# A list scheduler and GpSimd substitution in the first phase of a hybrid decoder layer

## The chip, the core and the metric

The program runs on one core of a Trainium2 chip. A core has TensorE (matrix products and transposes, results in PSUM), VectorE, ScalarE, GpSimd and SyncE, which here only issues DMA. Each engine works its own queue in program order; semaphores tie the queues together. The metric is the device time of one launch in microseconds.

## The reference, cut

One decoder layer over 2048 tokens of width 1024. Its input projection has 26 tiles of 128 columns, for two groups of heads: eight RWKV-7 heads of 64 and four gated-linear-attention (GLA) heads. A SwiGLU feed-forward of width 2816 follows.

```python
def reference(x, rms1_g, w_in, ..., final_g):
    h = x
    for l in range(DEPTH):                      # DEPTH = 1
        n = rms_norm(h, rms1_g[l])
        z = n @ w_in[l]
        y_rwkv = rwkv7_mixer(z[..., :D_RWKV_IN], ...)
        y_gla = gla_mixer(z[..., D_RWKV_IN:], gk_up[l], gk_bias[l], gla_norm_g[l])
        mix = jnp.concatenate([y_rwkv, y_gla], axis=-1).astype(h.dtype)
        h = h + mix @ w_out[l]
        n = rms_norm(h, rms2_g[l])
        h = h + (jax.nn.silu(n @ ffn_gate[l]) * (n @ ffn_up[l])) @ ffn_down[l]
    return rms_norm(h, final_g)

# rwkv7_mixer, per token and head: the state S is 64 x 64
    sa = jnp.einsum('bhvk,bhk->bhv', S, a_t)
    S = (S * w_t[:, :, None, :] + sa[..., None] * b_t[:, :, None, :]
         + v_t[..., None] * k_t[:, :, None, :])
    y = jnp.einsum('bhvk,bhk->bhv', S, r_t)
```

Both kernels take the recurrence in chunks of 64 tokens: inside a chunk a triangular system (I - E) X = R is solved, and the state goes from chunk to chunk.

## The kernel before

Phase A works on four blocks of 512 tokens. In a block the rows are normed and transposed (`nprep`), split into a high and a low part, and multiplied with 26 tiles of the input projection (`zmm`, three matmuls for each of eight slices of the channels, L381 to L383; result `zd`). The weights of a tile come by DMA and are split by ScalarE (`w_hi`, L371) and GpSimd (`w_lo`, L372), twice 512 columns each.

Two heads lie on the 128 partitions together, so a block has four head pairs, sixteen in all. Each goes through three streams:

- `stage_a`: decay, keys, scores. Its masked scores are `e` (L539) and `ra` (L541).
- `stage_a2`: solves the triangular systems. Four 32-partition transposes (L597) spread the diagonal 32 x 32 blocks of `e` into `ln`; 31 steps of a multiply and an add (L606, L608) on VectorE invert them into `lm`, the sizes from 31 columns over 76 down to 8; a transpose makes `ui` (L626). Six groups of small matmuls and the moves of their results follow (`xu` L640, `xy` L648, `xl` L657, two of each); VectorE adds `xy` to `R` (L653), ScalarE copies the others (L644, L661). At the end `ar` is written (L667).
- `stage_b`: the chain over eight chunks. For each: matmul `yp` (L693), VectorE `uv` (L695), matmul `ch` (L700), VectorE `S` (L703, two halves), and so on to the next chunk. Then group norm and gate.

The GLA group has `glaz` and `gmix`. Five Python generators are merged by `run` (a heap ordered by time estimates that the generators give as they yield), and the scheduler of the framework then orders the instructions of each engine by its own estimates; once built, the order is fixed. PSUM has the tags `zd`, `ma` and `mb` with two banks each and `yp` and `ch` with one.

Phase B is the output projection with residual (L964 to L966) and the feed-forward (`up`, `down`), in three matmuls for each product, too. In its first part it uses what phase A leaves free.

## Time and profile before

| | us |
|---|---|
| median of 3 runs | 3006.15 |
| lowest, highest | 3003.69, 3013.07 |
| span of the profiled execution, first to last instruction | 3011.3 |
| last matmul of the input projection starts | 1282.4 |
| last state step of `stage_b` (L703) starts | 1361.0 |

The profiled execution has no other time than its span; the span is within the range of the three runs and 5 us above their median. In the rows below, busy time is the time in which an engine shows at least one instruction; for TensorE the ends of matmuls are modelled, so starts are safer than ends. PEld is TensorE's weight load. The granted clock is given as a share of full speed: TensorE has two levels, 1.2 and 2.4 GHz, so a number between 0.5 and 1.0 is a mixture of both over the stretch.

### The profile page before, as it was taken

How to read it: one execution, taken by the hardware profiler on the slowest of the kernel's cores; microseconds unless marked ns; L12 is line 12 of the kernel's file. 1: busy time of each engine (PE TensorE's matmuls, PEld its weight loads, DVE VectorE, ACT ScalarE, POOL GpSimd, SP SyncE). 2: the span in 40 equal slices, each digit the busy share in tenths (PEclk: the TensorE clock that was granted, in tenths of full speed). 3: DMA queues.
4: the chain of work that ended last, by engine and by line, in shares of the span. 5: the costliest groups of instructions: out<-in, count | busy, mean ns of one | idle time of the engine just before them, and what ended most of it. 6: DMA issues, size and time to landing. Idle time of an engine off the chain costs nothing.

```text
span 3011.3 us, 38996 instructions
## 1 busy us (share of the span) xinstructions
PE 2871.0 (95%) x15112; PEld 2247.0 (75%) x15112; DVE 1732.7 (58%) x3990; ACT 953.1 (32%) x1718; POOL 344.2 (11%) x451
## 2 busy tenths in 40 slices
PE   7898999899898989899999999999999999999998
PEld 5676677666666767668878888888888888888886
DVE  6868797888888897874433333333355333333334
ACT  5444445444445445332321111111132111111112
POOL 4222232213322222200000000000000000000000
PEclk9999989989999999989999999999999999999999
DMA  3122111221122111135531111111134111111111
GB/s 108 48 71 78 50 53 47 78 67 56 53 67 81 53 53 50 57 114 175 180 119 45 54 42 42 50 55 50 42 126 138 52 42 42 51 54 50 42 42 57
DMA packets 99033, 206.08 MB, mean 68 GB/s; under 512 B 8608, under 2 KB 41600, under 8 KB 98848
## 3 DMA queue, kind: packets, MB, share of 16 engines
q1 hardware_dynamic: 98848, 203.59, 21.7%
q8 instruction: 119, 1.95, 0.3%
q14 instruction: 66, 0.54, 0.1%
HBM read 178.39 MB, written 25.17 MB: 68 GB/s over the span
## 4 chain that ended last, share of the span: by engine, by line
PE 76%; DVE 20%; issue 2%; ACT 1%; DMA 1%; POOL 0%; SPq 0%; DVEq 0%; ACTq 0%; POOLq 0%
PE ups L995 5%; PE ups L996 5%; PE gps L996 5%; PE gps L997 5%; PE gps L995 5%; PE ups L997 5%; PE dn L1018 5%; PE dn L1019 5%; PE dn L1017 5%; DVE ln L597 3%; PE zd L383 3%; DVE lm L608 3%; PE zd L381 3%; PE zd L382 3%; DVE lt L606 3%
## 5 line engine op out<-in xcount | busy, mean ns | idle before, releaser
L381 PE MATMUL zd<-nh,w_hi 128*128 128x512 f32 x832 | 353.9, 426 | 0.8 <-DVE gkk L777 0.6
L383 PE MATMUL zd<-nh,w_lo 128*128 128x512 f32 x832 | 349.2, 420 | 0.0
L1020 DVE TENSOR_TENSOR h<-dn,h 128x512 f32<-128x512 f32 x352 | 242.7, 690 | 180.6 <-PE dn L1019 180.5
L382 PE MATMUL zd<-nl,w_hi 128*128 128x512 f32 x832 | 345.6, 415 | 0.0
L372 POOL TENSOR_TENSOR w_lo<-w_raw,w_hi 128x512 fp32r<-128x512 f32 x208 | 273.8, 1322 | 614.5 <-ACT w_hi L371 571.8
L1000 DVE TENSOR_TENSOR sgu<-sgu,ups 128x512 f32<-128x512 f32 x88 | 60.2, 684 | 392.6 <-PE ups L997 390.4
L1018 PE MATMUL dn<-wdl,hh 128*128 128x512 f32 x704 | 278.4, 395 | 0.0
L996 PE MATMUL gps<-n2l,wgh 128*128 128x512 f32 x704 | 278.2, 395 | 0.0
L995 PE MATMUL gps<-n2h,wgh 128*128 128x512 f32 x704 | 277.6, 394 | 0.4 <-ACT wgh L901 0.4
L996 PE MATMUL ups<-n2l,wuh 128*128 128x512 f32 x704 | 278.0, 395 | 0.0
L995 PE MATMUL ups<-n2h,wuh 128*128 128x512 f32 x704 | 277.7, 394 | 0.2 <-ACT wuh L901 0.2
L1019 PE MATMUL dn<-wdh,hl 128*128 128x512 f32 x704 | 277.7, 395 | 0.0
L997 PE MATMUL gps<-n2h,wgl 128*128 128x512 f32 x704 | 277.4, 394 | 0.0
L997 PE MATMUL ups<-n2h,wul 128*128 128x512 f32 x704 | 277.4, 394 | 0.0
L1017 PE MATMUL dn<-wdh,hh 128*128 128x512 f32 x704 | 277.4, 394 | 0.0
L901 ACT CAST wdh<-raw 128x1024 fp32r<-128x1024 f32 x44 | 46.4, 1053 | 462.5 <-PE dn L1019 250.5
L383 PEld LDWEIGHTS zd<-nh,w_lo 128*128 128x128 f32 x832 | 161.6, 194 | 35.7 <-issue 7.5
L381 PEld LDWEIGHTS zd<-nh,w_hi 128*128 128x128 f32 x832 | 162.5, 195 | 33.2 <-issue 5.2
L382 PEld LDWEIGHTS zd<-nl,w_hi 128*128 128x128 f32 x832 | 161.9, 195 | 33.3 <-issue 7.9
L371 ACT CAST w_hi<-w_raw 128x512 fp32r<-128x512 f32 x208 | 126.3, 614 | 130.9 <-PE zd L382 83.7
L999 ACT ACTIVATE sgu<-gps 128x512 f32<-128x512 f32 x88 | 52.7, 599 | 339.4 <-PE gps L997 339.4
L995 PEld LDWEIGHTS gps<-n2h,wgh 128*128 128x128 f32 x704 | 132.1, 188 | 33.0 <-ACT wgh L901 0.9
(244 smaller groups left out, 5111.9 us busy)
## 6 DMA issues: line engine op xcount, KB each, us to landing
w_raw<-in_win SPq DMA_DIRECT2D x208, 256.0 KB, 2.7
raw<-in_wg SPq DMA_DIRECT2D x44, 512.0 KB, 4.2
raw<-in_wu SPq DMA_DIRECT2D x44, 512.0 KB, 3.6
raw<-in_wd SPq DMA_DIRECT2D x44, 512.0 KB, 3.6
xk<-in_x SPq DMA_DIRECT2D x16, 512.0 KB, 4.6
raw<-mix SPq DMA_DIRECT2D x16, 512.0 KB, 3.6
hx<-in_x SPq DMA_DIRECT2D x16, 512.0 KB, 3.6
hs<-hx SPq DMA_DIRECT2D x16, 512.0 KB, 2.9
```

The source lines that it names most:

```text
L371: nc.scalar.copy(out=whi[:, ks, :], in_=raw)
L372: nc.gpsimd.tensor_tensor(out=wlo[:, ks, :], in0=raw, in1=whi[:, ks, :].bitcast(F32), op=ALU.subtract)
L381: nc.tensor.matmul(out=ps, lhsT=whi[:, k, :], rhs=self.nh[k], start=(k == 0), stop=False)
L382: nc.tensor.matmul(out=ps, lhsT=whi[:, k, :], rhs=self.nl[k], start=False, stop=False)
L383: nc.tensor.matmul(out=ps, lhsT=wlo[:, k, :], rhs=self.nh[k], start=False, stop=(k == KT - 1))
L995: nc.tensor.matmul(out=ps, lhsT=w[0][:, ks], rhs=h, start=(k == 0), stop=False)
L996: nc.tensor.matmul(out=ps, lhsT=w[0][:, ks], rhs=l, start=False, stop=False)
L997: nc.tensor.matmul(out=ps, lhsT=w[1][:, ks], rhs=h, start=False, stop=(k == KT - 1))
L1017: nc.tensor.matmul(out=ps, lhsT=hh[:, ts], rhs=wd[f][0][:, ds], start=(f == 0), stop=False)
L1018: nc.tensor.matmul(out=ps, lhsT=hh[:, ts], rhs=wd[f][1][:, ds], start=False, stop=False)
L1019: nc.tensor.matmul(out=ps, lhsT=hl[:, ts], rhs=wd[f][0][:, ds], start=False, stop=(f == 1))
L1020: nc.vector.tensor_tensor(out=H[t][:, ds], in0=ps, in1=H[t][:, ds], op=ALU.add)
```

## The change

Three things are done together, all in phase A.

**The order.** `Order` replaces `run` and the framework's scheduler for this phase (`tc.manual_schedule()`). It emits nine streams: `b`, `a2`, `e` (results of the projection out of PSUM), `w` (weights), `x` and `p` (rows, normed and transposed), `a`, `g`, and `z` (projection matmuls) as the filler. After each emitted piece it reads the new instructions, gives each a duration by a formula for engine, operation and size, and keeps when each engine is free and each tile written and read. The stream with the earliest time goes next; the filler's time is TensorE's. `Slots` does the same book-keeping for buffers that are used again. The tiles of the projection follow one list, `SEQZ`, in which RWKV and GLA tiles alternate.

**Buffers and banks.** PSUM: `zd` 2, `ma` 2, `mb` 1 for `stage_a2`, `mg` 1 for GLA under a lock, `yp` and `ch` 1 each, also used for the end of `stage_b`. The three buffers `b4` become two of `xb` and one of `bk`; `Pm` becomes three buffers with a memset for each head pair; `tb` has two instead of three. In phase B `ups` alternates between the two banks `mb` and `mg`.

**The substitution.** The four transposes become one: ScalarE first packs the four diagonal blocks into `ed` (four copies of 32 x 256), then VectorE transposes 128 x 1024 at once into `ln` (L936). The 62 steps of a head pair run on GpSimd (L952, L954). GpSimd also writes an identity into the lower diagonal block of `e` of each chunk once `ed` and `upp` have read it (L971), so that the `xy` matmul over all 64 rows gives the sum with `R`, and ScalarE copies it out where VectorE added.

```diff
+class Order:
...
+    def run(self, streams):
+
+        q = [[0.0, n, name, gen, filler] for n, (name, gen, filler) in enumerate(streams)]
+        waiting = {}
+        while q:
+            pe = self.free.get("PE", 0.0)
+            s = min(q, key=lambda s: (max(s[0], pe - 50.0) if s[4] else s[0], s[1]))
...
-        self.run()
+        with tc.manual_schedule():
+            self.order = Order(nc)
+            self.s, s0 = self.order.pool(self.s), self.s
+            self.pp, p0 = self.order.pool(self.pp), self.pp
+            self.order.take()
+            self.order.run(self.streams())
...
+    SEQZ = [ZL, ZK, ZR, ZV, ZQ, ZKG, ZVG, ZK + 1, ZR + 1, ZV + 1, ZVG + 1, ZG, ZOG, ZK + 2, ZR + 2, ZV + 2, ZOG + 1,
+            ZQ + 1, ZKG + 1, ZK + 3, ZR + 3, ZV + 3, ZVG + 2, ZVG + 3, ZOG + 2, ZOG + 3]
...
+        return [("b", each(self.stage_b, HP), False), ("a2", each(self.stage_a2, HP), False),
+                ("e", self.evac(nb), False), ("w", self.weights(nb), False), ("x", self.rows(nb), False), ("p", self.prep_a(nb), False),
+                ("a", each(self.stage_a, HP), False), ("g", each(self.gmix, 2), False),
+                ("z", self.zmm(nb), True)]
...
     def stage_a2(self, b, hp):
...
-        ln = s.tile([128, 32, 32], F32, name="ln", bufs=1)
+
+        ed = s.tile([128, 32, 8], F32, name="ed", tag="lt", bufs=1)
         for q in range(4):
             par, t0 = q // 2, 32 * (q % 2)
             ev = e.rearrange("p h a x t -> p (h a) x t")[32 * q:32 * q + 32, :, par, t0:t0 + 32]
-            nc.vector.transpose(out=ln[32 * q:32 * q + 32],
-                                in_=ev.rearrange("p a t -> p t a").unsqueeze(2).to_broadcast([32, 32, 4, 8]))
-        yield 4.0
+            nc.scalar.copy(out=ed[32 * q:32 * q + 32], in_=ev.rearrange("p a t -> p t a"))
+        yield
+        ln = s.tile([128, 32, 32], F32, name="ln", bufs=1)
+        nc.vector.transpose(out=ln, in_=ed.unsqueeze(2).to_broadcast([128, 32, 4, 8]))
...
         for j in range(31, 0, -1):
             i0 = j // 4
             n = 8 - i0
-            nc.vector.tensor_tensor(out=lt[:, 0:j, i0:], in0=lm[:, j:j + 1, i0:].to_broadcast([128, j, n]),
+            nc.gpsimd.tensor_tensor(out=lt[:, 0:j, i0:], in0=lm[:, j:j + 1, i0:].to_broadcast([128, j, n]),
                                     in1=ln[:, j, 0:j].unsqueeze(2).to_broadcast([128, j, n]), op=ALU.mult)
-            nc.vector.tensor_tensor(out=lm[:, 0:j, i0:], in0=lm[:, 0:j, i0:], in1=lt[:, 0:j, i0:], op=ALU.add)
-            yield 0.6
...
+            nc.gpsimd.tensor_tensor(out=lm[:, 0:j, i0:], in0=lm[:, 0:j, i0:], in1=lt[:, 0:j, i0:], op=ALU.add)
+            yield
...
+                for par in range(2):
+                    q = slice(64 * par + 32, 64 * par + 64)
+                    nc.gpsimd.tensor_copy(out=e.rearrange("p h a x t -> p (h a) x t")[q, :, par, 32:64],
+                                          in_=self.ident[q, q].unsqueeze(1).to_broadcast([32, 8, 32]))
...
-                Rg = R[lw(par), 2 * g:2 * g + 2]
-                nc.vector.tensor_tensor(out=Rg, in0=ps[lw(par)], in1=Rg, op=ALU.add)
-            yield 1.5
+                nc.scalar.copy(out=R[lw(par), 2 * g:2 * g + 2], in_=ps[lw(par)])
+            yield
```

How the instructions stand. VectorE, between two steps of a chunk chain (`uv`, `S`) in the third block, before: the substitution of another head pair (`lt`, `lm`) stands between them.

```order
L695 TENSOR_TENSOR uv<-yp,R 64x128
L608 TENSOR_TENSOR lm<-lm,lt 128x29
L606 TENSOR_TENSOR lt<-lm,ln 128x28
L608 TENSOR_TENSOR lm<-lm,lt 128x28
L606 TENSOR_TENSOR lt<-lm,ln 128x27x2
L703 SCALAR_TENSOR_TENSOR S_0_112<-ch,Pm_122,st 64x64 x2
L608 TENSOR_TENSOR lm<-lm,lt 128x27x2
```

VectorE at such a place after, also in the third block.

```order
L1062 SCALAR_TENSOR_TENSOR S_1_101<-ch,Pm,st 64x64 x2
L1051 TENSOR_TENSOR uv<-yp,R 64x128
L633 SCALAR_TENSOR_TENSOR k<-zd,om,sh 128x512
L1062 SCALAR_TENSOR_TENSOR S_0_100<-ch,Pm,st 64x64 x2
L1071 TENSOR_TENSOR y<-yp,y 64x256 x2
L1169 TENSOR_TENSOR gat<-gsc,cst 128x512
```

The substitution steps are gone from between `uv` and `S`; what stands there are results of the projection, GLA scores and norms.

VectorE around `ui` in the third block, before: the transposes of the next head pair (`ln`) stand around it, and the substitution that ends in `ui` is on the same engine.

```order
L608 TENSOR_TENSOR lm<-lm,lt 128x16
L606 TENSOR_TENSOR lt<-lm,ln 128x8
L608 TENSOR_TENSOR lm<-lm,lt 128x8
L597 STREAM_TRANSPOSE ln<-e 32x1024
L626 STREAM_TRANSPOSE ui<-lm 128x32x8
L597 STREAM_TRANSPOSE ln<-e 32x1024 x3
L606 TENSOR_TENSOR lt<-lm,ln 128x31
L608 TENSOR_TENSOR lm<-lm,lt 128x31
```

VectorE around a `ui` after; `k` and `bk` are keys of the head pair that follows, `ar` its scaled rows.

```order
L836 TENSOR_TENSOR bk<-k_7371,pinv 128x4x128
L843 TENSOR_TENSOR ar<-kk,Pm 128x4x128
L844 TENSOR_TENSOR ar<-r,Pm 128x4x128
L974 STREAM_TRANSPOSE ui<-lm 128x32x8
L861 TENSOR_TENSOR e<-scp,cst 128x4x64
L863 TENSOR_TENSOR ra<-scp,cst 128x256
```

`ui` now takes `lm` from another engine, and the scores `e` and `ra` of the following head pair stand behind it.

GpSimd in the middle of the first phase, before: the last column of each projection tile is carried over (`cr`, `sh`), weights are split, `uv` is cleared, and `lm` is set up for a substitution that runs on VectorE.

```order
L393 COPY cr<-sh 128x1
L372 TENSOR_TENSOR w_lo<-w_raw,w_hi 128x512
L390 COPY sh<-cr 128x1
L562 MEMSET uv 64x2x128
L563 MEMSET uv 64x2x128
L601 COPY lm<-cst 128x256
```

GpSimd at the sixth substitution after.

```order
L952 TENSOR_TENSOR lt<-lm,ln 128x27x2
L954 TENSOR_TENSOR lm<-lm,lt 128x27x2
L952 TENSOR_TENSOR lt<-lm,ln 128x26x2
L954 TENSOR_TENSOR lm<-lm,lt 128x26x2
L567 TENSOR_TENSOR w_lo<-w_raw,w_hi 128x512
L952 TENSOR_TENSOR lt<-lm,ln 128x25x2
L954 TENSOR_TENSOR lm<-lm,lt 128x25x2
L952 TENSOR_TENSOR lt<-lm,ln 128x24x2
L954 TENSOR_TENSOR lm<-lm,lt 128x24x2
L567 TENSOR_TENSOR w_lo<-w_raw,w_hi 128x512
```

The steps now stand in GpSimd's queue, with the weight splits of the projection between them.

## Rows read from the trace of the kernel before

**Rows 1.** Page, whole span: busy time, share and instructions of each engine.

```profile
span 3011.3 us, 38996 instructions
PE 2871.0 (95%) x15112; PEld 2247.0 (75%) x15112; DVE 1732.7 (58%) x3990; ACT 953.1 (32%) x1718; POOL 344.2 (11%) x451
```

**Rows 2.** Windows by stage: length, busy us (instructions) of each engine, clock, DMA share, GB/s.

```profile
26.50:1282.80 1256.30, 1150.28 (x7516) 865.53 (x7514) 1018.21 (x2676) 580.32 (x1109) 336.40 (x420) 0.95 0.20 61
1282.80:1371.20 88.40, 82.48 (x489) 59.56 (x489) 62.43 (x206) 32.16 (x64) 0.61 (x2) 0.88 0.39 122
1371.20:3011.30 1640.10, 1628.36 (x7071) 1314.82 (x7069) 632.58 (x1066) 326.09 (x511) 0.00 (x0) 1.00 0.22 70
```

**Rows 3.** Timeline, TensorE: start, length, engine, line, operation, tiles, count.

```profile
703.33 0.40 PE L383 MATMUL zd<-nh,w_lo 128*128 128x512 f32 x1
...
704.03 0.40 PE L383 MATMUL zd<-nh,w_lo 128*128 128x512 f32 x1
...
1255.83 1.06 PE L657 MATMUL xl<-R,ui 32*32 32x128 f32 x16
1256.82 0.50 PE L381 MATMUL zd<-nh,w_hi 128*128 128x512 f32 x1
...
1262.18 0.60 PE L549 MATMUL bkp<-ident,bk 128*128 128x128 f32 x4
1262.61 0.39 PE L693 MATMUL yp<-S,ar 128*128 128x128 f32 x2
```

**Rows 4.** By line: ns min/median/max, first and last start (us).

```profile
L597 DVE STREAM_TRANSPOSE ln<-e x64: 1902/1977/2027, 64.5 to 1267.2; 32x1024 f32<-32x1024 f32 x64
...
L626 DVE STREAM_TRANSPOSE ui<-lm x16: 612/673/749, 113.1 to 1319.4; 128x256 f32<-128x256 f32 x16
...
L667 ACT COPY ar<-wtp x16: 577/586/588, 134.4 to 1338.2; 128x512 f32<-128x512 f32 x16
```

**Rows 5.** Waits, 0 to 1290 us: us in sum, times, longest.

```profile
PEld ch L706 <- DVE S L703: 46.8, 86, 1.9
```

**Rows 6.** Windows of 50 us in the first stage, columns as in rows 2.

```profile
150.00:200.00 50.00, 50.00 (x366) 37.73 (x366) 29.04 (x69) 28.94 (x53) 14.08 (x17) 1.00 0.21 59
...
400.00:450.00 50.00, 42.63 (x223) 33.91 (x221) 45.96 (x121) 22.49 (x39) 15.18 (x18) 0.83 0.16 48
```

**Rows 7.** Groups by line, VectorE: busy us, mean ns, idle before.

```profile
L606 DVE TENSOR_TENSOR lt<-lm,ln 128x60 f32<-128x60 f32 (+24 forms) x496 | 136.9, 276 | 10.8
...
L608 DVE TENSOR_TENSOR lm<-lm,lt 128x60 f32<-128x60 f32 (+24 forms) x496 | 136.3, 275 | 10.3
...
L597 DVE STREAM_TRANSPOSE ln<-e 32x1024 f32<-32x1024 f32 x64 | 126.4, 1975 | 1.2
...
L653 DVE TENSOR_TENSOR R<-xy,R 32x512 f32<-32x512 f32 x64 | 44.2, 690 | 29.8 <-PE xy L648 28.3
```

**Rows 8.** Groups by line, ScalarE: the copy of `xl`.

```profile
L661 ACT COPY R<-xl 32x512 f32<-32x512 f32 x64 | 37.0, 578 | 61.3 <-PE xl L657 57.2 <-DVE lt L606 3.3
```

**Rows 9.** Groups by line, GpSimd; below them, from the timeline, two memsets in a row.

```profile
L372 POOL TENSOR_TENSOR w_lo<-w_raw,w_hi 128x512 fp32r<-128x512 f32 x208 | 273.8, 1322 | 614.5 <-ACT w_hi L371 571.8 <-PE ch L700 30.8 <-PE zd L383 4.2
...
L390 POOL COPY sh<-cr 128x1 f32<-128x1 f32 x52 | 10.5, 202 | 26.6 <-DVE k L398 9.7 <-DVE r L398 8.1 <-DVE v L444 6.6
...
L601 POOL COPY lm<-cst 128x256 f32<-128x256 f32 x16 | 6.5, 407 | 45.6 <-DVE ui L626 29.4 <-DVE rn_y L113 7.2 <-DMA cst<-in_cst 6.8
...
716.20 0.30 POOL L562 MEMSET uv<- 64x256 f32 x1 [3.67 <-PE ch L706]
...
716.56 0.31 POOL L563 MEMSET uv<- 64x256 f32 x1
```

**Rows 10.** Timeline, GpSimd and VectorE around 1190 us.

```profile
1190.19 0.16 DVE L91 TENSOR_TENSOR gr_t<-gr_y 128x4 f32<-128x4 f32 x1
...
1190.62 1.29 POOL L575 TENSOR_TENSOR prl<-pr,prh 128x512 fp32r<-128x512 f32 x1 [4.42 <-ACT prh L574]
...
1190.78 1.15 DVE L91 TENSOR_TENSOR gr_t<-gr_y 128x4 f32<-128x4 f32 x1
```

More of the change, by code (lines that the diff above doesn't have):

```diff
@@ L293, in nstat0 @@
         r = self.rsqrt(s1, NPR, "rn0")
[L294 to L295 removed]
+        return [r[:, j:j + 1] for j in range(NPR)]
     def nstat(self, b):
@@ L375, in zmm @@
-    def zmm(self, ct):
-        nc = self.nc
-        whi, wlo = self.ahead.pop(0) if self.ahead else self.weights(ct)
-        ps = self.pp.tile([128, BLK], F32, name="zd", bufs=2)
-        for k in range(KT):
-            nc.tensor.matmul(out=ps, lhsT=whi[:, k, :], rhs=self.nh[k], start=(k == 0), stop=False)
-            nc.tensor.matmul(out=ps, lhsT=whi[:, k, :], rhs=self.nl[k], start=False, stop=False)
-            nc.tensor.matmul(out=ps, lhsT=wlo[:, k, :], rhs=self.nh[k], start=False, stop=(k == KT - 1))
-        return ps
+                yield f"pt{b - 1}.{KT // 2 - 1}"
@@ new lines, in zmm @@
+    def zmm(self, nb):
+        nc = self.nc
+        self.zps = {}
+        for b in range(nb):
+            for i in range(NZ):
+                yield f"w{b}.{i}"
+                if i > 1:
+                    yield f"ze{b}.{i - 2}"
+                else:
+                    yield f"prep{b}.{KT // 2 - 1}" if i else f"pt{b}.{KT // 2 - 1}"
+                    if not i:
+                        yield f"prep{b}.{KT // 2 - 2}"
+                whi, wlo = self.wz.pop((b, i))
+                ps = self.zd("zd", [128, BLK])
+                for k in range(KT):
+                    if not i and not k % 2:
+                        yield f"prep{b}.{k // 2}"
+                    nh, nl = self.nhl[b, k]
+                    nc.tensor.matmul(out=ps, lhsT=whi[:, k, :], rhs=nh, start=(k == 0), stop=False)
+                    nc.tensor.matmul(out=ps, lhsT=whi[:, k, :], rhs=nl, start=False, stop=False)
+                    nc.tensor.matmul(out=ps, lhsT=wlo[:, k, :], rhs=nh, start=False, stop=(k == KT - 1))
+                    if i == NZ - 1 and k % 2:
+                        yield ("set", f"zk{b}.{k // 2}")
+                    else:
+                        yield
+                self.zps[b, i] = ps
+                yield ("set", f"zm{b}.{i}")
@@ L566, in stage_a @@
             uv.append(t)
-        yield 2.0
+        yield
+        self.bb[n] = [None, None, uv]
+        yield ("set", f"uv{n}")
+        bkt = []
+        for g in range(2):
+            ps = self.ma("bkp", [128, 4, 128])
+            for i in range(4):
+                nc.tensor.transpose(out=ps[:, i, :], in_=bkc(g * 4 + i), identity=self.ident)
+            yield
+            t = s.tile([128, 4, 128], F32, name="bkt", bufs=3)
+            nc.scalar.copy(out=t, in_=ps)
+            bkt.append(t)
+            yield
         pr = self.ta("pr")
         nc.vector.scalar_tensor_tensor(out=pr, in0=r, scalar=col(V_RK), in1=k2, op0=ALU.mult, op1=ALU.mult)
+        yield
         bp = self.ma("bp", [128, BLK])
@@ L704, in stage_b @@
                                                in1=st[hq, hq], op0=ALU.mult, op1=ALU.add)
-            for h in range(2):
-                nc.tensor.matmul(out=yu[nq, j % 2, 64 * h:64 * h + 64], lhsT=ra[par][:, h, j, :],
-                                 rhs=uvc[:, 64 * h:64 * h + 64], start=True, stop=True)
+            yield
             if c % 4 == 3:
@@ L822, in gmix @@
-        nc.gpsimd.tensor_copy(out=SS[:, 0, :], in_=SG)
-        yield 3.0
+            yield
+            if not par:
+                d = self.tg("gd0").rearrange("p (a d) -> p a d", d=128)
+                nc.scalar.copy(out=d, in_=ps)
+                yield
+                ps = d
+            dps.append(ps)
         for c in range(NCH):
```

865 lines of the change are left out of this document (556 added, 309 removed).

## The prediction

> **What bounds the kernel now.** The page first: TensorE is shown 95% busy, VectorE 58% of the whole span [rows 1]. The windows by stage say that the two halves of the program differ. From 1371 us on (output projection and feed-forward) TensorE is busy for 1628.4 of 1640.1 us; nothing in the change touches that stage's work. From 26.5 to 1282.8 us (first matmul to last projection matmul) TensorE shows 1150.3 of 1256.3, VectorE 1018.2, ScalarE 580.3, GpSimd 336.4 [rows 2]. All of the change lies there and in the 88 us after it.
>
> TensorE's share must not be believed in that first stage: ends of matmuls are modelled. Projection matmuls that follow each other start 0.233 us apart (three steps in 0.70 us) although each is shown as 0.40 [rows 3]. So I work out what TensorE needs. 2496 projection matmuls x 0.233 = 582 us. All its records are 15112 [rows 1]; less these 2496, and less 7360 of the second stage (9 lines x 704, 3 x 256, and 256 transposes of `prep`), 5256 small ones are left. About 3584 of them are of the short forms (`xu`, `xy`, `xl`, `upp`, `ra`, `scp`, `gds`, `gop`); a group of 16 takes 0.99 us from its start to the next group's, 0.062 each: 222 us. The other 1672 go at a transpose's 0.108 (four in 0.43): 181 us [rows 3]. Together 985 us, or **62 us for each of the 16 head pairs** (4 blocks x 4).
>
> What they take now comes from the substitution stream `stage_a2`. It runs its 16 head pairs one after another with single buffers `ln`, `lm`, `lt`, `ui`. The first `ln` transpose starts at 64.5 us and the last `ar` copy ends at 1338.2 + 0.6: 1274.3 / 16 = **79.6 us a head pair** [rows 4]. Why so long: its substitution stands in VectorE's queue between everything else, the first one from 64.5 to 113.1 us, and the six matmul steps behind it take some 20 us (first: 113.1 + 0.7 to 134.4 + 0.6 is 21.2; last: 1319.4 + 0.7 to 1338.2 + 0.6 is 18.7) [rows 4]. VectorE is the loaded engine and TensorE waits for it: the longest wait of its weight loads, 46.8 us in sum, is for `S`, a step of `stage_b`'s chain that stands among substitution steps in VectorE's queue [rows 5]. TensorE also loses clock: in a 50 us stretch with 42.6 us busy it was granted 0.83, so between its two levels, in one with 50.0 it had the full one [rows 6]. Slack costs twice.
>
> **Part by part.** *VectorE* loses the 2 x 496 substitution steps (136.9 + 136.3 us), 48 of 64 transposes (126.4 x 3/4 = 94.8) and the 64 adds of `xy` (44.2) [rows 7]: 412 of the 1081 us of two windows [rows 2]. The 669 that stay are 42 us a head pair; it stops being the bound. *ScalarE* gets 64 packing copies, 64 `xy` copies and eight `gd0`, 0.58 us each at most, the price of an `xl` copy of twice the packing copy's columns [rows 8]: 79 us on 612, 43 us a head pair, behind TensorE's 62. *TensorE* gets and loses next to nothing.
>
> *GpSimd* gets 992 two-input steps. Such small ones are not in this trace. The price: one-input copies take 0.20 us for one column and 0.41 for 256, so 0.19 is fixed, a little under the first; `w_lo` takes 1.32 for 512, so (1.32 - 0.19) / 512 = 2.2 ns a column [rows 9]. One substitution has 2 x 1560 columns in 62 steps: 62 x 0.19 + 3120 x 2.2 ns = 18.6 us. Each step waits for the one before it on the same engine; such a pair, the two memsets, shows 0.06 us between end and start [rows 9]: 3.7 us more. So 22.3 us, 0.36 a step (an estimate). Bounds: not under the 17 us of VectorE's 62 x 0.276 [rows 7]; above, the first rival.
>
> Now the new cycle of one head pair, from the order of the changed program: four packing copies 1.5 (between half a copy's price and a whole), one transpose 2.0, hand-overs 1: 4.5, where 4 x 1.98 stood; steps 22.3; between them in GpSimd's queue on average 5.4 `w_lo`, one `prl` and some ten short copies and memsets, 11; the port (below) 6; `ui` with its hand-over 1; the matmul steps 20. Sum **64.8 us**. That is 3 above TensorE's 62, and two loads so equal on queues in program order will wait for each other now and then; I add 2 and take **67**.
>
> *The port.* GpSimd and VectorE exclude each other: while GpSimd ran `prl` (from 1190.62, 1.29 us) a VectorE step of 4 columns took 1.15 instead of 0.16 us [rows 10]. VectorE's steps with two inputs from the same memory, in one head pair: seven of 512 columns at 0.69, a scan as two of these, some 35 small ones at 0.16, 2 us of others: 13.8 us [rows 7, 10]. Half of the cycle is substitution, so GpSimd loses about 6 us in it; the ends are 0 and 13.8.
>
> *New waits.* `ui` on VectorE now waits for GpSimd; behind it in VectorE's queue stand the `e` and `ra` steps of the next head pair, and TensorE's `scp` waits for those. `w_lo` stands behind substitution steps in GpSimd's queue; behind it wait projection matmuls, two column tiles ahead. GpSimd's own sum a head pair is 22.3 + 13 x 1.34 + 1.3 + some 4 = 45 us, 51 with the port, under 67: that cover holds, and if it were gone each us over 67 would count in full. The fixed order costs nothing by itself: projection matmuls stand in threes between the chain's steps in both programs. The renamed banks and buffers of the second stage keep their counts.
>
> Sum: 16 x (79.6 - 67) = 202 us. The profiled execution spans 3011.3 [rows 1]; 3011.3 - 202 = 2809. The median of the runs, 3006.15, is 5 below that span: **2804 us**.
>
> **Rivals.** *1. The GpSimd step is slow (slower than before).* GpSimd's `w_lo` takes 1.32 us where VectorE's `xy` add takes 0.69 for as many columns [rows 7, 9], a factor of 1.9. If short steps keep that factor instead of a fixed part and a slope, a step is 1.9 x 0.276 + 0.06 = 0.58 us, 0.22 above mine: 67 + 13.6 = 80.6 us, **3022 us**. For it: rows of one to eight columns with a broadcast operand are in no row. Against: GpSimd's copies of one column at 0.20. It decides from 0.36 + 12.6 / 62 = 0.56 us a step from start to start on. Chance 0.13. The Trainium skill, GPSIMD Engine Reference, section Engine selection, has a rule of this kind against the change: elementwise work with two inputs belongs on VectorE, GpSimd being about twice as slow. By that rule a step would be some 0.61 us with the hand-over and the time some 3052 us, an estimate; the trace agrees at 512 columns and shows nothing at these sizes.
>
> *2. The port takes all.* The 13.8 us are lost in full, and the `ui` that comes late holds VectorE: 67 + 7.8 = 74.8 us a head pair, **2929 us**. For it: [rows 10], and GpSimd will be at work three quarters of this stage instead of one quarter [rows 2]. Against: VectorE has room. Chance 0.17.
>
> *3. The order undoes it.* Wherever the fixed order guesses a step shorter than it is, TensorE stands, and the cycle stays within 0.6 us of 79.6: **3006 us**. Then the change does not do what it says. Against: the order before was fixed as well once built. Chance 0.05.
>
> *4. Only TensorE is left.* 62 us a head pair: **2724 us**. The substitution stream would have to hide wholly. Chance 0.10.
>
> **How the numbers follow.** Forecast, 63 to 72 us a head pair, 2740 to 2884 us: 0.55. With rival 2 up to 76 us a head pair (2948) and rival 4 down to 2720 the range, 2720 to 2950, holds a little over 0.8. Faster by over 0.3% (about what a measurement of this kernel can tell from no change): 0.55 + 0.17 + 0.10 = 0.82; within 0.3%: 0.05; slower: 0.13.
>
> **What would show it.** Right: from the first `ln` transpose to the end of the last `ar` copy 63 to 72 us a head pair; VectorE's busy time in the first stage 350 us lower or more; a step on GpSimd near 0.3 us; TensorE's longest wait no longer `S`; a granted clock above 0.95 in that stage; the second stage still 1640 us. Wrong: GpSimd steps of 0.5 us (rival 1); VectorE steps of two inputs that take 1 us in number (rival 2); projection matmuls at 0.233 us, no waits, and yet over 72 us a head pair: then my count of TensorE's small matmuls is off.

## The result, and the profile of the changed kernel

The changed kernel takes 3046.09 us (median of four runs, 3043.28 to 3050.17) beside 3008.74 us for the one before (3003.69 to 3013.07): ratio 1.0115, 95% interval 1.0091 to 1.0139. It is slower by 37 us, 1.2%; the prediction was 2804.

The engines changed as foreseen. The page of the changed kernel, busy time and instructions of each engine (before: [rows 1]):

```profile
span 3045.3 us, 39060 instructions
...
PE 2866.3 (94%) x15112; PEld 2268.3 (74%) x15112; DVE 1392.5 (46%) x2886; ACT 1031.9 (34%) x1854; POOL 647.2 (21%) x1489
```

By stage, columns as in [rows 2]: first the whole first stage, then a stretch between two blocks, a stretch inside a block, and the second stage.

```profile
26.50:1319.00 1292.50, 1154.10 (x7581) 887.53 (x7581) 690.67 (x1634) 661.80 (x1251) 633.78 (x1450) 0.94 0.19 59
...
308.60:351.70 43.10, 32.73 (x263) 24.58 (x261) 27.87 (x79) 18.76 (x36) 16.31 (x47) 0.80 0.23 69
...
421.00:644.50 223.50, 206.05 (x1407) 158.95 (x1405) 108.00 (x248) 113.73 (x216) 125.32 (x296) 0.95 0.17 50
...
1405.00:3045.30 1640.30, 1628.93 (x7082) 1319.32 (x7080) 635.32 (x1076) 326.75 (x513) 0.00 (x0) 1.00 0.22 70
```

VectorE lost 328 us of the first stage, GpSimd gained 297, the second stage still takes 1640 us. The first stage is longer all the same: the last projection matmul starts at 1311.1 us instead of 1282.4. Where the time went is seen when the substitution stream is followed from head pair to head pair. Timeline of VectorE, the `ln` transposes of the first five head pairs after the change, with the `ui` of the first:

```profile
87.34 1.25 DVE L936 STREAM_TRANSPOSE ln<-ed 128x1024 f32<-128x1024 f32 x1 [1.03 <-ACT ed L933]
...
123.22 0.67 DVE L974 STREAM_TRANSPOSE ui<-lm 128x256 f32<-128x256 f32 x1 [3.10 <-POOL lm L954]
...
153.81 1.25 DVE L936 STREAM_TRANSPOSE ln<-ed 128x1024 f32<-128x1024 f32 x1 [0.51 <-ACT ed L933]
...
230.44 1.25 DVE L936 STREAM_TRANSPOSE ln<-ed 128x1024 f32<-128x1024 f32 x1 [2.31 <-ACT ed L933]
...
295.00 1.25 DVE L936 STREAM_TRANSPOSE ln<-ed 128x1024 f32<-128x1024 f32 x1
...
420.99 1.25 DVE L936 STREAM_TRANSPOSE ln<-ed 128x1024 f32<-128x1024 f32 x1 [1.03 <-ACT ed L933]
```

The same in the kernel before, the first of the four `ln` transposes of each head pair:

```profile
64.47 1.96 DVE L597 STREAM_TRANSPOSE ln<-e 32x1024 f32<-32x1024 f32 x1
...
111.19 1.99 DVE L597 STREAM_TRANSPOSE ln<-e 32x1024 f32<-32x1024 f32 x1
...
207.27 1.95 DVE L597 STREAM_TRANSPOSE ln<-e 32x1024 f32<-32x1024 f32 x1
...
283.86 1.97 DVE L597 STREAM_TRANSPOSE ln<-e 32x1024 f32<-32x1024 f32 x1
...
391.45 1.93 DVE L597 STREAM_TRANSPOSE ln<-e 32x1024 f32<-32x1024 f32 x1
```

After: 66.5, 76.6, 64.6 us inside the block and 126.0 over its border. Before: 46.7, 96.1, 76.6 and 107.6. The table sums these intervals over the whole stage (12 ordinary, 3 over borders); with the start of the first `ln` and the time from the last `ln` to the end of the last `ar` copy they add up to the end of the stream. All kernels of this study stand in it; an ordinary interval lies inside a block, and ratios are to the kernel before on the same chip (its median differs by up to 7 us from chip to chip, so small differences between rows go by the ratios). The kernels are explained under Experiments.

| kernel | median us | ratio (95%) | first `ln` | 12 ordinary, sum (mean) | 3 borders, sum | last pair |
|---|---|---|---|---|---|---|
| before | 3008.74 | | 64.5 | 872.5 (72.7) | 321.1 | 80.7 |
| after | 3046.09 | 1.0115 (1.0091-1.0139) | 87.3 | 833.4 (69.5) | 374.2 | 69.0 |
| zcut | 3045.54 | 1.0112 (1.0078-1.0146) | 86.7 | 852.0 (71.0) | 345.5 | 71.7 |
| subcut | 2979.08 | 0.9891 (0.9870-0.9912) | 84.6 | 771.8 (64.3) | 375.0 | 47.6 |
| noprep | 2931.23 | 0.9738 (0.9712-0.9763) | 83.5 | 817.3 (68.1) | 274.2 | 68.9 |
| e_bank | 3000.50 | 0.9957 (0.9942-0.9971) | 91.1 | 825.0 (68.7) | 342.1 | 66.1 |
| h80 | 3030.45 | 1.0061 (1.0046-1.0076) | 84.5 | 830.6 (69.2) | 370.7 | 66.2 |
| r_dep | 2969.58 | 0.9867 (0.9848-0.9886) | 87.4 | 832.9 (69.4) | 301.1 | 69.9 |
| d60 | 2987.79 | 0.9911 (0.9882-0.9940) | 87.4 | 855.7 (71.3) | 302.0 | 63.0 |
| d80 | 2984.75 | 0.9909 (0.9879-0.9940) | 88.5 | 841.1 (70.1) | 313.3 | 71.5 |
| r_pe | 3012.13 | 0.9990 (0.9973-1.0007) | 87.9 | 825.1 (68.8) | 348.8 | 62.6 |
| r_port | 3046.92 | 1.0126 (1.0103-1.0149) | 82.2 | 963.8 (80.3) | 257.2 | 59.7 |
| r_port2 | 3007.08 | 0.9981 (0.9971-0.9992) | 81.1 | 952.6 (79.4) | 238.6 | 57.3 |
| e_bankdep | 2957.79 | 0.9823 (0.9806-0.9840) | 89.5 | 851.8 (71.0) | 270.1 | 68.0 |
| r_vec | 3114.59 | 1.0349 (1.0329-1.0369) | 86.4 | 887.1 (73.9) | 388.8 | 74.9 |
| b_sub | 3159.65 | 1.0495 (1.0470-1.0520) | 68.3 | 986.0 (82.2) | 337.1 | 82.1 |
| a_free | 3128.11 | 1.0386 (1.0361-1.0411) | 79.3 | 919.9 (76.7) | 374.2 | 72.1 |
| b_pack | 3009.45 | 0.9984 (0.9971-0.9998) | 69.5 | 870.4 (72.5) | 320.3 | 70.2 |
| a_wlo | 3002.56 | 0.9965 (0.9948-0.9982) | 79.7 | 817.5 (68.1) | 367.1 | 65.4 |
| best1 | 2935.15 | 0.9748 (0.9721-0.9775) | 82.3 | 796.2 (66.3) | 316.7 | 61.7 |

From before to after: start +23, ordinary -39, borders +53, last pair -12, together +25 us of the span's +34 (9 more come behind the stream). So 76 us were lost at the start and the borders, and 51 won elsewhere.

What happens at a border. Timeline of TensorE after the change: the last projection matmul of the first block, groups of four transposes `tch` of the next block's rows (the first group stood at 304 us, three more lie in the lines left out), two of the waits, and the first projection matmul of the next block.

```profile
308.55 0.39 PE L593 MATMUL zd<-nh,w_lo 128*128 128x512 f32 x1
...
315.79 0.60 PE L527 MATMUL tch<-ident,xk 128*128 128x128 f32 x4
...
320.01 1.09 PE L1196 MATMUL gotp<-ident,gon 128*128 128x128 f32 x4 [3.40 <-DVE gon L1191]
...
324.37 1.06 PE L527 MATMUL tch<-ident,xk 128*128 128x128 f32 x4
...
326.11 0.66 PE L527 MATMUL tch<-ident,xk 128*128 128x128 f32 x4
...
337.71 0.63 PE L1196 MATMUL gotp<-ident,gon 128*128 128x128 f32 x4 [2.23 <-DVE gon L1191]
...
349.32 0.72 PE L527 MATMUL tch<-ident,xk 128*128 128x128 f32 x4
...
351.66 0.50 PE L591 MATMUL zd<-nh,w_hi 128*128 128x512 f32 x1
```

For 43.1 us no projection matmul runs; TensorE is shown busy for 32.7 of them, with the small matmuls of the chains, and its granted clock falls to 0.80. In the kernel before this stretch is 13.4 us:

```profile
306.56 0.40 PE L383 MATMUL zd<-nh,w_lo 128*128 128x512 f32 x1
...
313.33 1.91 PE L331 MATMUL tch<-ident,xk 128*128 128x128 f32 x8
...
320.04 0.48 PE L381 MATMUL zd<-nh,w_hi 128*128 128x512 f32 x1
```

There `tch` has the two banks `ma`, and the next block's projection starts once its first slices are there. In the change `tch` shares the two banks of `zd` with the projection, and `zmm` lets a block's first matmul go only when all eight slices are transposed (`pt`). The slices also come more slowly: at this border the eight groups start between 4.5 us ahead of the block's last projection matmul and 40.8 us behind it, in the kernel before between 6.8 and 18.7 us behind it. All three borders show the gap (43, 42 and 43 us; before 13, 16 and 13), and so does the start: the first projection matmul of the program comes at 33.6 us instead of 18.3.

The gap accounts for the longer borders. Each border is cut at the last projection matmul of the old block and at the first of the new one. From the fourth `ln` to the last matmul, over the gap, and from the first matmul to the next `ln`, the three borders have 68, 43 and 210 us before and 41, 129 and 205 after: the gap is 86 us longer, and 33 of them come back at its two sides.

TensorE's longest waits, 0 to 1330 us, are no longer for `S` ([rows 5]) but for the norms of `stage_b` (`ytp`) and of GLA (`gotp`). The three numbers are us in sum, times, longest:

```profile
PE ytp L1093 <- DVE y L1086: 37.6, 13, 5.1
PE gotp L1196 <- DVE gon L1191: 26.2, 14, 3.4
```

They lie inside the blocks: of the 37.6 us for `ytp` only 2 fall into the three gaps.

### The profile page after: what moved, and what is told of

Its sections match the earlier page's. It is cut to its first block, busy times and chain, and to the rows that moved or that the text cites. A ratio compares the mean times of both kernels' runs of the same rounds, so it can differ in the third digit from the quotient of the medians.

```text
span 3045.3 us, 39060 instructions
## 1 busy us (share of the span) xinstructions
PE 2866.3 (94%) x15112; PEld 2268.3 (74%) x15112; DVE 1392.5 (46%) x2886; ACT 1031.9 (34%) x1854; POOL 647.2 (21%) x1489
## 4 chain that ended last, share of the span: by engine, by line
PE 80%; DVE 8%; ACT 4%; POOL 4%; issue 2%; DMA 1%; SPq 0%; POOLq 0%; DVEq 0%; ACTq 0%
PE ups L1333 5%; PE gps L1333 5%; PE ups L1331 5%; PE dn L1354 5%; PE dn L1353 5%; PE ups L1332 5%; PE gps L1332 5%; PE gps L1331 5%; PE dn L1355 5%; PE zd L591 5%; PE zd L592 4%; PE zd L593 4%; PE op L1300 2%; PE op L1301 2%; PE op L1302 2%
## 5 line engine op out<-in xcount | busy, mean ns | idle before, releaser
L591 PE MATMUL zd<-nh,w_hi 128*128 128x512 f32 x832 | 373.3, 449 | 0.7 <-DVE nl L538 0.3
L593 PE MATMUL zd<-nh,w_lo 128*128 128x512 f32 x832 | 335.2, 403 | 9.8 <-POOL w_lo L567 9.8
L592 PE MATMUL zd<-nl,w_hi 128*128 128x512 f32 x832 | 333.8, 401 | 0.0
L593 PEld LDWEIGHTS zd<-nh,w_lo 128*128 128x128 f32 x832 | 160.9, 193 | 50.7 <-POOL w_lo L567 13.4
L954 POOL TENSOR_TENSOR lm<-lm,lt 128x60 f32<-128x60 f32 (+24 forms) x496 | 162.4, 327 | 38.8
L1331 PEld LDWEIGHTS ups<-n2h,wuh 128*128 128x128 f32 x704 | 132.5, 188 | 31.9 <-ACT wuh L1237 1.3
```

The costliest lines, as they stand in the source:

```text
L591: nc.tensor.matmul(out=ps, lhsT=whi[:, k, :], rhs=nh, start=(k == 0), stop=False)
L592: nc.tensor.matmul(out=ps, lhsT=whi[:, k, :], rhs=nl, start=False, stop=False)
L593: nc.tensor.matmul(out=ps, lhsT=wlo[:, k, :], rhs=nh, start=False, stop=(k == KT - 1))
L954: nc.gpsimd.tensor_tensor(out=lm[:, 0:j, i0:], in0=lm[:, 0:j, i0:], in1=lt[:, 0:j, i0:], op=ALU.add)
L1331: nc.tensor.matmul(out=ps, lhsT=w[0][:, ks], rhs=h, start=(k == 0), stop=False)
```

## Experiments

Four theories stood against each other. A: the plan's lengths of short steps are too short, and TensorE stands where they are wrong. B: GpSimd's steps themselves cost the time. C: any fixed order loses what the framework's scheduler had. D: the loss sits at the block borders.

**What sets the cycle: three kernels that leave work out.** All three start from the changed kernel; as in every run here that keeps the list scheduler, the plan is made anew.

zcut, without the low part of the projection weights:

```diff
-                    nc.tensor.matmul(out=ps, lhsT=wlo[:, k, :], rhs=nh, start=False, stop=(k == KT - 1))
```

> The changed kernel without the third matmul of each projection product (low part of the weights times high part of the rows): 832 of 2496 projection matmuls are left out, 194 us at 0.233 each. If the sum of TensorE's work and of its stands sets the cycle, the time falls by 150 to 200 us, to 2850 to 2900. If the streams' own chains set it (the plan, made anew, ends only 47 us earlier), by 30 to 60 us, to 2985 to 3015.

Measured 3045.54 us: nothing, less than either side had it. 194 us of TensorE's work are gone and the stream's ordinary head pair takes 71.0 us instead of 69.5. The window of its first stage, columns as above:

```profile
26.50:1319.00 1292.50, 1064.44 (x6818) 793.27 (x6817) 705.98 (x1653) 663.63 (x1259) 642.55 (x1461) 0.86 0.19 60
```

TensorE is shown 90 us less busy than in the changed kernel, and its granted clock is 0.86 instead of 0.94: TensorE's sum of work does not set this stage's length. How much the lower clock and the new plan took back of a gain is not taken apart by a run.

subcut, half of the substitution:

```diff
-        for j in range(31, 0, -1):
+        for j in range(15, 0, -1):
```

> The changed kernel without the first 16 of the 31 double steps of each substitution (32 of 62 GpSimd steps are left out). If the substitution stream sets the ordinary head pair: ln to ui falls from 36 to 45 us to 25 to 33, an ordinary interval from 69.5 to 56 to 61, and the time by 12 x 10 us or more, to 2880 to 2930. If TensorE or the chain over the chunks sets it: intervals stay at 66 to 70 and the time within 20 us of 3046. The planner's own view: 4 us less, since by it TensorE is the bound.

Measured 2979.08, between the two. The first two `ln` and the `ui` between them:

```profile
84.56 1.25 DVE L936 STREAM_TRANSPOSE ln<-ed 128x1024 f32<-128x1024 f32 x1 [1.03 <-ACT ed L933]
...
103.73 0.67 DVE L974 STREAM_TRANSPOSE ui<-lm 128x256 f32<-128x256 f32 x1 [3.23 <-POOL lm L954]
...
138.76 1.25 DVE L936 STREAM_TRANSPOSE ln<-ed 128x1024 f32<-128x1024 f32 x1
```

From `ln` to `ui` 19.2 us, where the changed kernel has 35.9, over all head pairs 21 instead of 39. Of these 18 us the ordinary interval gives back only 5 (69.5 to 64.3): the stream now stands 6 to 39 us between its last transposes `wtp` and the next `ln` (4 to 9 in the changed kernel), until the scores of the next head pair are there. So the supply of scores is not much faster than the substitution was; the borders stay at 375. The planner's own view (4 us) missed the 67 us, too.

noprep, without the preparation of the rows of blocks 1 to 3:

```diff
+                if b:
+                    yield f"ze{b - 1}.{NZ - 1}"
+                    for i in range(2):
+                        self.nhl[b, 2 * kp + i] = self.nhl[0, 2 * kp + i]
+                    yield ("set", f"pt{b}.{kp}")
+                    yield ("set", f"prep{b}.{kp}")
+                    continue
```

> The changed kernel without the preparation of the rows of blocks 1 to 3 (loads, norm, scaling, 96 transposes tch, their copies are left out; the projection uses the rows of block 0 again). If the preparation sets the border: the gap without projection matmuls falls from 43 to under 8 us, a border interval from 125 to 75 to 90, the time by 105 to 150 us, to 2895 to 2940. If the border is set by the chain over the chunks of the last head pair and by the streams behind it: the gap closes, but the border intervals stay over 100 us and the time over 2985.

Measured 2931.23, 115 us less. The gap without projection matmuls is 7.5 us (first two lines below), ordinary intervals stay at 68.1, and the border, from the fourth `ln` to the fifth, is 91.5:

```profile
304.37 0.40 PE L598 MATMUL zd<-nh,w_lo 128*128 128x512 f32 x1
...
311.90 0.50 PE L596 MATMUL zd<-nh,w_hi 128*128 128x512 f32 x1
```

```profile
290.91 1.25 DVE L941 STREAM_TRANSPOSE ln<-ed 128x1024 f32<-128x1024 f32 x1
...
382.44 1.25 DVE L941 STREAM_TRANSPOSE ln<-ed 128x1024 f32<-128x1024 f32 x1 [0.84 <-ACT ed L938]
```

So the preparation, with its place in this order, costs about 33 us at each border (374.2 less 274.2, by three), and the shorter gap (23 us in sum instead of 129) covers all of it. The 23 us by which a border is still longer than an ordinary interval are not taken apart by a run.

**The banks at the border.** e_bank: `tch` takes only the bank that the last but one projection tile leaves; the next block's first tile takes the other and starts with the first slices. For this the two banks `zd` get names of their own, in the second stage too, and each slice's low part follows its high part.

```diff
-                    if b and not kp:
-                        yield f"ze{b - 1}.{NZ - 2 + i}"
-                    ps = self.zd("tch", [128, BLK])
+                    if b and not kp and not i:
+                        yield f"ze{b - 1}.{NZ - 2}"
+                    ps = self.zd("tch", [128, BLK], b + 1)
...
-                else:
-                    yield f"prep{b}.{KT // 2 - 1}" if i else f"pt{b}.{KT // 2 - 1}"
-                    if not i:
-                        yield f"prep{b}.{KT // 2 - 2}"
+                elif i:
+                    yield f"prep{b}.{KT // 2 - 1}"
+                elif b:
+                    yield f"ze{b - 1}.{NZ - 1}"
```

> The changed kernel; at the border of two blocks the eight transposes tch of the next block use one of the two zd banks, the one that the last but one projection tile leaves, and the next block's first projection tile takes the other bank and starts as soon as its first slices are there (in the change tch uses both banks, and no projection matmul may start until all eight are written). Theory D (the loss sits at the three block borders: in the change 43 us pass between the last projection matmul of a block and the first of the next, 13 to 16 before, and TensorE has no filler there): the gap falls to 5 to 15 us, 3 x 30 us are won, 3046 goes to 2940 to 2975. Theory A (lengths of the plan alone): 3025 to 3060, since they are unchanged. Chance alone: within 30 us of 3046.

Measured 3000.50: 46 us won, half of what the theory of the border gave. The gap is 8.8 us, but the first tile now takes 25 to 28 us from its first to its last matmul (7.3 in the changed kernel), since its slices still come one by one; gap and tile together fell from 50 to 35 us, three times 15. The mechanism holds, the price was doubled by looking at the gap alone. Last and first projection matmul at the first border, and the fourth and fifth `ln`, 115.4 us apart:

```profile
315.17 0.40 PE L590 MATMUL zd<-nh,w_lo 128*128 128x512 f32 x1
...
323.94 0.48 PE L588 MATMUL zd<-nh,w_hi 128*128 128x512 f32 x1
```

```profile
299.68 1.25 DVE L933 STREAM_TRANSPOSE ln<-ed 128x1024 f32<-128x1024 f32 x1
...
415.05 1.24 DVE L933 STREAM_TRANSPOSE ln<-ed 128x1024 f32<-128x1024 f32 x1
```

**The lengths in the plan.** r_dep: in the plan a step waits for the end of a step of its own engine that it reads.

```diff
-                    t = max(t, w[0] + (self.HOP if w[1] != e else 0.0) if w[1] != e else t)
+                    t = max(t, w[0] + (self.HOP if w[1] != e else 0.0))
```

> The changed kernel; one line of the planner is other: a step that reads what the same engine wrote starts, in the plan, no earlier than the end of the writing step (the plan of the change lets it start after the engine's hold, 0.083 us for a step of 8 columns on VectorE where the trace shows 0.20 us from start to start). Theory A (the plan guesses short dependent steps too short, and TensorE, whose order is fixed by it, stands at ytp, 39 us in all, gotp, 29 us, and xu, 16 us): these three waits fall to a half or less, 3046 goes to 2960 to 3015. Theory B (the substitution on GpSimd itself is what costs: the shared port and the w_lo steps between): no change, 3036 to 3056. Theory C (a fixed order of any kind loses what the framework's scheduler had): no change, 3036 to 3056.

Measured 2969.58, 77 us less, as theory A had it; of the three waits only `ytp` fell clearly (37.6 to 9.6 us in sum; `gotp` 26.2 to 19.8, `xu` 12.2 to 13.6). The wait for `ytp` in r_dep, 0 to 1330 us:

```profile
PE ytp L1093 <- DVE y L1086: 9.6, 8, 2.4
```

In the table the ordinary intervals are the same (832.9 to 833.4), and the borders lost 73 us. But only 46 of these are the gap (129 to 83 us over three borders). 21 more lie ahead of it: a block's projection takes 278 us from its first to its last matmul instead of 287 (means of four), and so ends earlier beside the stream. That TensorE's shorter waits for `ytp` inside the blocks make it so is likely, but no run shows it alone.

Is it the truer length, or one plan by luck? The changed kernel and r_dep with one number of the plan moved a little:

```diff
-    HOP = 70.0
+    HOP = 80.0
```

> The changed kernel with one number of the plan other, the delay from engine to engine, 0.080 us for 0.070: no length gets truer by it to speak of, the plan is only made anew. It tells how far two plans of the same quality lie apart. Its plan has the borders of the blocks 27 us long, the plan of the change 31. Theory A and theory D: 3020 to 3060. If each new plan falls anywhere: as far off as r_pe, under 3015, or over 3080.

> r_dep with 0.080 us for 0.070 as the delay from engine to engine in the plan. If the truer lengths of dependent steps give the 77 us: 2960 to 2985. If r_dep's plan is a lucky one: 2995 to 3035, with ordinary intervals of 68 to 71 us and longer borders (planned gaps at the borders: 29, 30, 22 us, where r_dep has 23, 25, 22).

> r_dep with 0.060 us. If truer lengths give the 77 us: 2960 to 2985. If luck: 2995 to 3035, again with ordinary intervals of 68 to 71 us (planned gaps at the borders: 30, 22, 29 us).

Without the true length 3046 and 3030 us, with it 2970, 2985 and 2988. Two plans of the same quality lie up to 18 us apart; the 58 us between the means of the two groups stand clear of that, with three plans against two. All three have borders of 301 to 313 us, not 371 to 374, and waits for `ytp` of 9 to 10 us in sum, not 38 and 28; `gotp` is 28 us in d60 and d80, no less than in the changed kernel. In these two the gap gives only 21 us and the earlier end of the block's projection the larger part.

r_pe adds TensorE's own length of small matmuls; r_port adds to r_dep that VectorE and GpSimd exclude each other (second diff), and r_port2 adds that to r_pe, with planned gaps used:

```diff
-                if w.shape[0] <= 64:
-                    h *= 0.6
-                if m <= 64:
+                if w.shape[0] <= 64 or m <= 64:
```

```diff
+            shared = e == "Pool" and len(ra) > 1 or e == "DVE" and not any(x in self.psum for x in ra)
+            if shared:
+                t = max(t, self.port)
+                self.port = t + hold
```

> r_dep with one more length of the plan mended: the factor 0.6 for small matmuls is taken once and not twice (xu, xy, xl and gds are planned at 0.079 us each, 0.63 for a group of eight, where the trace shows 0.99). The plan for the first phase grows from 1069 to 1129 us, 65.7 us a head pair. Theory A (too short lengths in the plan): TensorE is planned later behind each such group, its partners are less often late, r_dep's 2970 goes to 2925 to 2965. Rival (TensorE's own lengths don't matter, since its order stays about the same): 2965 to 2980. Rival (each new plan falls by chance within some 30 us): anything from 2940 to 3000, and no wait that shrinks for a reason.

> As r_dep, and the plan also keeps VectorE's steps without a PSUM source and GpSimd's steps with two sources apart in time. Its plan for one head pair is 70.7 us where that of the change is 61.2. Theory A: a plan nearer to what happens leaves TensorE fewer waits than r_dep's: 2930 to 3000. Theory B: TensorE's waits stay, 3030 or more. Theory C: 3030 or more.

> r_pe, and in the plan a VectorE step without a PSUM source and a GpSimd step with two sources don't overlap (gaps between planned steps are used, which r_port's plan couldn't). Plan 71.8 us a head pair. Theory A: VectorE's delays behind w_lo are planned for, TensorE waits less than in r_pe, 2900 to 2960. Rival (a plan that is too careful leaves TensorE planned idle, as in r_port): 3000 to 3060.

Measured 3012.13, 3046.92 and 3007.08: theory A fails here, and r_pe lies above all that was forecast for it, although it has r_dep's line. It has short ordinary intervals (68.8) but borders of 349. Both port plans have the shortest borders (257 and 239), and ordinary intervals of 80 us, with 53 and 50 us from `ln` to `ui` instead of 39; that the plan holds back steps that would have run is likely, but not shown. A truer length does not make a better order by itself; why r_pe's borders came out longer is open.

**Who gains by GpSimd.** r_vec is the changed kernel with the 62 steps on VectorE:

```diff
-            nc.gpsimd.tensor_tensor(out=lt[:, 0:j, i0:], in0=lm[:, j:j + 1, i0:].to_broadcast([128, j, n]),
+            nc.vector.tensor_tensor(out=lt[:, 0:j, i0:], in0=lm[:, j:j + 1, i0:].to_broadcast([128, j, n]),
...
-            nc.gpsimd.tensor_tensor(out=lm[:, 0:j, i0:], in0=lm[:, 0:j, i0:], in1=lt[:, 0:j, i0:], op=ALU.add)
+            nc.vector.tensor_tensor(out=lm[:, 0:j, i0:], in0=lm[:, 0:j, i0:], in1=lt[:, 0:j, i0:], op=ALU.add)
```

b_sub is the kernel before with the lines of `stage_a2` from the change's diff alone, b_pack the same with these two steps left on VectorE; a_free is the changed kernel with the order left to the framework:

```diff
-        with tc.manual_schedule():
+        if True:
```

> The changed kernel with the 62 substitution steps of a head pair on VectorE instead of GpSimd, packed transpose and fixed order kept; the planner plans anew by its own formula. Theory A: the same stands of TensorE at ytp and gotp, VectorE some 250 us more loaded, 3020 to 3080. Theory B: without GpSimd's steps the port is free and the substitution takes 17 us instead of 24: under 3000. Theory C: 3030 to 3060.

> The kernel before, its streams and its scheduler, with the substitution of the change alone: four packing copies and one transpose for four transposes, the 62 steps on GpSimd, xy with an identity block so that ScalarE copies it. Theory A (the loss sits in the plan of the change): faster than before, 2920 to 2990. Theory B (it sits in GpSimd's steps): 3010 to 3070. Theory C: 2800 to 2920, what the prediction gave for the whole change.

> The kernel before with the packed transpose and the identity block of xy alone; the 62 steps stay on VectorE, order by the framework's scheduler as before. If b_sub lost its 152 us by the steps on GpSimd (VectorE's ui stood 18.5 us each time for GpSimd, with the chain's steps behind it): 2960 to 3000, since VectorE loses 139 us of work. If the scheduler's order falls badly with any change of this stream: 3020 or more.

> The changed kernel, its nine streams and its GpSimd substitution, but the order of the first phase is left to the framework's scheduler, as before the change (the planner still writes the program down in its order). Theory A (the plan's lengths are what loses): the framework's own estimates decide, 2980 to 3100, with ui on VectorE standing for GpSimd as in b_sub if they are short for GpSimd, too. Theory C (a fixed order loses what a scheduler had): under 2960.

In the fixed order GpSimd is worth 68 us (3114.59 to 3046.09), the contrary of theory B. Under the framework's scheduler it costs 150 (3009.45 to 3159.65), and the packing alone is worth nothing. r_vec, b_sub and a_free are slower than any theory had them. The waits of VectorE, 0 to 1500 us, in b_sub:

```profile
DVE ui L632 <- POOL lm L609: 288.7, 16, 25.3
```

and in a_free:

```profile
DVE ui L974 <- POOL lm L954: 236.3, 16, 19.9
```

The scheduler sets `ui` into VectorE's queue so early that VectorE stands 18 us (b_sub) and 15 us (a_free) on average before GpSimd is done, sixteen times; in 9 and 12 of them a `uv` or `S` of the chain is the first or second step behind it. In the changed kernel all these waits sum to 20 us. So the list scheduler is worth 82 us with the substitution on GpSimd (3128.11 to 3046.09).

With it on VectorE the order costs. b_pack and r_vec have the same steps on every engine but for eight copies on ScalarE and 14 memsets on GpSimd, and differ by the order, the banks and the buffers: 3009.45 to 3114.59, 105 us, of which 68 lie in the borders. Put in a row, these runs take the change apart: the packing nothing, order, banks and buffers together 105 us lost, GpSimd in that order 68 won. How the 105 divide between the three no run shows; a_free has the banks of the change and gaps of 26.5 us, so the banks alone do not make the changed kernel's 43.

**Both remedies.** a_wlo is the changed kernel with `w_lo` on VectorE, best1 the same with the banks of e_bank and the line of r_dep; e_bankdep has these two alone.

```diff
-                    nc.gpsimd.tensor_tensor(out=wlo[:, ks, :], in0=raw, in1=whi[:, ks, :].bitcast(F32), op=ALU.subtract)
+                    nc.vector.tensor_tensor(out=wlo[:, ks, :], in0=raw, in1=whi[:, ks, :].bitcast(F32), op=ALU.subtract)
```

> The changed kernel with w_lo (13 steps a head pair of 1.3 us on GpSimd) on VectorE, 0.69 us each there. If w_lo among the substitution steps and the port lengthen the ordinary cycle (5 to 6 of them lie within a substitution): ln to ui falls to 28 to 36 us, ordinary intervals to 59 to 64, the time by 60 to 130 us, to 2915 to 2985. If VectorE, with 143 us more, becomes late for the chain's steps: no gain or a loss, 3030 to 3080.

> r_dep (a step that reads what its own engine wrote waits in the plan for the end of it) with the banks of e_bank. Theory D: r_dep's gap of 26 to 29 us at each border falls to 5 to 15, 3 x 17 us, 2970 goes to 2905 to 2940. If r_dep was faster only because its borders were shorter: the same as e_bank, 2940 to 2975. Theory A alone: 2955 to 2985.

> e_bankdep (2958) with w_lo on VectorE as in a_wlo. If the two add up: 2840 to 2900. If the plan made anew takes it back: 2940 or more.

a_wlo: from `ln` to `ui` 30 us instead of 39, but only 44 us won, and the stream again waits for the next scores (23 to 32 us from `wtp` to `ln` before the third head pair of each block). e_bankdep: 2957.79, short of 2905 to 2940; r_dep's borders had already become shorter, and the banks add 12 us. best1, 2935.15 us, ratio 0.9748 (0.9721 to 0.9775), beats both kernels, by 2.5 and 3.6%; it lies above the 2840 to 2900 hoped for.

## Why the prediction was wrong, step by step

**The cycle inside a block came out, in part by errors that cancel.** 64.8 + 2 = 67 us was forecast for a head pair; the 12 ordinary ones take 69.5. Its first part, a GpSimd step of 0.36 us from start to start, was forecast from copies and one large step, and it held (median 0.37); by line the steps take

```profile
L954 POOL TENSOR_TENSOR lm<-lm,lt 128x60 f32<-128x60 f32 (+24 forms) x496 | 162.4, 327 | 38.8
L952 POOL TENSOR_TENSOR lt<-lm,ln 128x60 f32<-128x60 f32 (+24 forms) x496 | 141.9, 286 | 52.9 <-DVE ln L936 27.1
```

0.31 on average, without hand-over. Steps, other work of GpSimd and port were 22.3 + 11 + 6 = 39.3 us; from the first step's start to the last one's end it is 36.3. The matmul steps behind `ui`, read from the first and the last head pair as 20 us, take 25.3: the same stretch took 18 to 49 us in the kernel before (26 in the mean), so two of sixteen were no fair sample. One term 3 us too high and one 5 too low leave the sum near, which is luck. Rivals 1 and 2 are out: no step near 0.56 us, and a cycle under 74.8. VectorE steps that take over 0.4 us more than the lower quartile of their kind number 63 in the first stage, 109 in the kernel before.

The rule of the Trainium skill (GPSIMD Engine Reference, section Engine selection: about twice as slow with two inputs) does not hold at 8 to 76 columns here; at 512 columns it does [rows 9]. The 0.276 us of VectorE [rows 7] are a mean that 58 steps of over 0.7 us raise; weighted medians by size are 0.215 us there and 0.292 on GpSimd, a factor of 1.36.

**The multiplier was wrong; this is the first step that failed.** "16 x (79.6 - 67)" took one mean from the first `ln` and the last `ar` [rows 4] and let all sixteen head pairs shrink alike. The 79.6 are 72.7 inside the blocks and 107 over the borders, which the trace of before shows when each `ln` is read. The forecast's stream ends at 64.5 + 16 x 67 = 1136.5 us, the real one at 1364.0. Of these 227 us, 173 are the borders (374.2 less 3 x 67), 29 the ordinary intervals (833.4 less 12 x 67), 23 the start, 2 the last pair. The 9 us behind the stream make up the rest of the miss in the span. With borders as before, cycles of 67 us could win only 12 x 5.7 = 68 us, and 14 at the last pair, not 202. By the sign that the prediction set itself, the time from the first `ln` to the last `ar` by sixteen, the cycle is 79.8 us, where it had been 79.6.

**"The fixed order costs nothing by itself" was wrong**, the second step that failed, and it gave the sign. With the substitution on VectorE, the order, banks and buffers of the change cost 105 us (b_pack to r_vec), more than the 68 that GpSimd wins in that order. It was argued from stretches inside a block. At the border the new order lets no projection matmul start before all eight slices are transposed, 43 us against 13 to 16. The text spoke of "the renamed banks" only for the second stage; the move of `tch` from `ma` to `zd` had no term. noprep (115 us, the whole preparation) bounds this loss, and e_bank (46) is what the banks and the starting rule are worth. r_dep (77) is in part another loss: 46 of it are the gap, and inside the blocks TensorE stands less for `ytp`. This is rival 3 in kind ("wherever the fixed order guesses a step shorter than it is, TensorE stands"); its 0.05 was far too low, and its price, "the cycle stays", had no loss in it.

**"TensorE 62 us a head pair" bounds nothing here.** zcut takes 12 us a head pair away and the time stays. The count may be good, no run tests it; that TensorE would be "the bound" behind which the streams hide was not.

**Right besides:** ScalarE +82 us (79), `ui` a small wait, TensorE's wait for `w_lo` 23 us in sum at most, `S` no longer its longest wait, 1640 us for the second stage. VectorE is 328 us lower in the first stage, a little short of the 350 that were asked. The clock above 0.95 did not come: 0.94, and 0.80 at the border. (26.5 us, from which the stage is counted, is not the first matmul: the first projection matmul of the kernel before starts at 18.3.)

## What to carry to other kernels

Before a cycle is multiplied by its count, read each of its turns in the trace: a mean over block borders hides that a faster step shortens only the turns between them. When a change renames banks or buffers, follow what fills the engine while they are handed over; here the start and the borders lost 76 us, more than the 51 won elsewhere. What a new order costs is measured by a run with the old work in it. A plan's lengths for short dependent steps can be worth nearly as much as an engine (58 us here beside 68), but a truer length did not always help, and it takes two or three plans of each kind to tell a cause from luck.
